# A hybrid encoder trunk in float32: seven-product pairs in one more stage, a wider attention-value product, fewer pages completed by DMA, and a new planner table

## The chip, the cores and the metric

The kernel runs on one core of a Trainium2 chip. The metric is the device time of one execution in microseconds; lower is better. Three runs of the kernel before gave 2622.74, 2623.55 and 2625.89 us, median 2623.55 us.

## The reference, cut to what matters

Two layers. In each, one input projection feeds grouped-query attention (16 query heads over 4 key/value heads) and eight bidirectional retention heads; both are gated and meet in one output projection with a residual:

```python
for l in range(DEPTH):                      # 2
    h = rmsnorm(x, norm_w[l])               # x: 256 x 4096, float32
    proj = h @ w_in[l]                      # 4096 x 11264
    aq, ak, av, ag, rq, rk, rv, rg = jnp.split(proj, SPLIT_POINTS, axis=-1)
    ...
    a_out = silu(ag) * gqa_attention(aq, ak, av)
    ...
    r_out = silu(rg) * rmsnorm(bidirectional_retention(...), ret_norm[l])
    x = x + jnp.concatenate([a_out, r_out], axis=-1) @ w_out[l]   # 4096 x 4096
return rmsnorm(x, final_norm)
```

Almost all arithmetic lies in `h @ w_in` and in the product with `w_out`; the weights, 256 rows of tokens against 4096 x 15360 numbers per layer, are read once from HBM.

## The kernel before, in words

**Stages and blocks.** Four stages follow each other: w_in of layer 0, w_out of layer 0, w_in of layer 1, w_out of layer 1 (stages 0 to 3). A w_in stage has 11 blocks, a w_out stage 4. A block makes two 512-wide column groups for all 256 tokens, so its result is a 2 x 2 arrangement of 128 x 512 tiles. The 4096 rows of the sum are taken as 16 pairs of 128-row slices.

**Products.** A pair would need eight 128 x 128 by 128 x 512 products for the 2 x 2 tiles. The pairs in `SEVEN` (0, 3, 6, 9, 12) need seven, by sums of operands and of weights (Strassen's scheme in Winograd's form, `SEVEN_PRODUCTS`); the pairs in `MORE` (before: pair 1) need seven in the w_out stages alone. All others take `EIGHT_PRODUCTS`. The partial results meet in PSUM banks M1 to M7, and `combine` (VectorE additions) puts the four tiles together at the end of a block. Blocks at the start of stage 0 counted by `PLAIN` use `PLAIN_PRODUCTS`, with an eighth bank M8; the difference operands (`third`: x3, the difference of the two token halves) are then not needed yet.

**Float32 by three products.** Every operand is split in a high part (a cast to float32r on ScalarE) and a low part (the rest, a subtraction on VectorE). A product is three matmuls: weights' high part with the operand's high and low part (line 1472), and weights' low part with the operand's high part (line 1482). `TOGETHER` products of one page run their high matmuls first, then the low ones.

**Weights.** A page is 128 x 1024 numbers of a pair. SyncE loads raw pages (`wraw`, 5 buffers); ScalarE makes `whi`, VectorE `wlo` (5 buffers each, `RING`). A seven-product pair has four pages: A, T, B, U, where T and U are sums of weights (`wsum`, one 1024-wide and two 512-wide VectorE operations per block), and B is half a page. An eight-product pair has pages A and B. For the pairs in `FAR_PAIRS` (before: 2, 5, 8, 11, 14, in every stage) page B's low part is made without VectorE: ScalarE writes `fhi` and then `flo` = -`fhi`, and GpSimd issues a DMA that adds the weights from HBM into `flo` (line 516). There is one `fhi`/`flo` buffer (`FAR = 1`), so the next far page can be begun only when the last product with the previous one is through.

**Other work.** Attention, retention, rotary embedding, the residual and the splitting of operands for the next stage are generators (`Lane`, `Turn`) whose steps are put between the products. `attention_values` (lines 1112 to 1138) is called 16 times, each for two heads.

**What sets the order.** Everything is written out at build time. After each product `tick` puts pending low parts, transfers and steps into the engines' queues if `Weights.room` says that VectorE and ScalarE will still be in time for the next pages. `room` reckons with the table at the file's head (`STEP_V`, `STEP_S`, `V_FIXED`, `PASS`, `MARGIN`, `RUSH`, `LANDING`, `ADD_AHEAD` and so on). The numbers therefore set only in which order instructions stand in each engine's queue; on the chip, semaphores alone decide when one starts.

Of the kernel before, what the change touches and what calls it, by code (L numbers as in the profile page):

```python
# [12 lines left out]
F32R = mybir.dt.float32r  # L13
# [4 lines left out]
P = 128  # L18
D_MODEL = 4096
SEQ = 256  # L20
DEPTH = 2
# [10 lines left out]
MT = SEQ // P  # L32
# [18 lines left out]
LANDING = 11.0  # L51
STORE = 7.0
FETCH = 13.0
FAR_LANDING = 11.0
MARGIN = 0.2

RUSH = 1.5

EARLY = 0.7

ADD_AHEAD = 2.5

NEED = {"ak": 4, "ag": 3, "rk": 4, "rg": 4}

PE_REST = 1.5

TIGHT_A = 4
TIGHT_B = 7

AT_ONCE = 2  # L70

WARM = 20

SPLITS = 3
# [10 lines left out]

WHOLE = 4

PLAIN = 2

DEFER = (0,)  # L90

FAR_PAIRS = (2, 5, 8, 11, 14)


AQ, AK, AV, AG, RQ, RK, RVO, RG = 0, 2048, 2560, 3072, 5120, 6144, 7168, 9216
# [95 lines left out]
    return order + rest  # L191


def is_far(group, p, k):

    return k == PAGE_B and p in FAR_PAIRS


def slots_of(group, second, first=False, plain=False):

    for _p, _k in pages_of(group, first):
        if _p in SEVENS[second] and not (first and _p in NATIVE):
# [11 lines left out]
EASY = ("M7",)  # L214


BANK_REST = 0.8
# [55 lines left out]
def hybrid_encoder(  # L273
# [136 lines left out]
    class Weights:  # L410


        def __init__(self):
            self.pages = []
            for l in range(DEPTH):
                for w, n in ((w_in, N_IN), (w_out, N_OUT2)):
                    for b in range(n):
                        second = w is w_out
                        for g in GROUPS[second]:
                            start = (l, b) == (0, 0) and w is w_in  # L420
                            for slot in slots_of(g, second, start):
# [3 lines left out]
                                one.seven = one.pair in SEVENS[second] and not one.whole  # L425
                                one.far = is_far(g, one.pair, one.kind) and not (
                                    start and (g in GROUPS[0][:2] or one.whole)
                                )
# [163 lines left out]
    def dead_room():  # L592

        if not rooms:
            e, o = len(EIGHTS), len(SEVENS[1])
# [32 lines left out]
    def split_pair(p, v, whole, stage):  # L628
# [12 lines left out]
                as_it_comes[p] = (whole, ac.until + PASS)  # L641
            yield
        x0, x1 = v[:, 0], v[:, 1]
        if p in SEVENS[stage % 2]:
# [5 lines left out]
            hi = t(ap, [P, 7, P], "x7h", len(SEVENS[1]), F32R)  # L650
            lo = t(ap, [P, 7, P], "x7l", len(SEVENS[1]), F32R)
# [16 lines left out]
        else:  # L668
            if p in EIGHTS:
                hi = t(ap, [P, 2, SEQ], "x8h", len(EIGHTS), F32R)  # L670
                lo = t(ap, [P, 2, SEQ], "x8l", len(EIGHTS), F32R)
                g = t(ap, [P, 2, 2, P], "x3", len(EIGHTS), F32R)
                g = [g[:, k] for k in range(2)]
            else:
                both = [t(ap, [P, 7, P], v, len(SEVENS[1]), F32R) for v in ("x7h", "x7l")]
# [23 lines left out]
        if p % 2:  # L699
            drop()  # L700
        version[p] += 1
        operand[p] = (hi, lo) if p in SEVENS[stage % 2] else (hi, lo, g)
        operand_at[p] = max(ve.until, ac.until) + PASS
        yield

# [264 lines left out]
        for m in range(MT):  # L970
            ve.tensor_sub(to[1][:, m], v[:, m], f32(to[0])[:, m])

    def in_both(v, i):

        return v.rearrange("p (k i t) -> p i k t", k=4 * MT, t=BLK)[:, i]

    def parts_of(name, shape):
        return page(shape, name + "h", F32R), page(shape, name + "l", F32R)

# [12 lines left out]
    def at(parts, *index):  # L992
        return [v[index] for v in parts]
# [121 lines left out]
    def attention_values(g, h, kv, sgT):  # L1115
# [17 lines left out]
        yield  # L1133
        drop(2)
        z = sgT.rearrange("p (k i t) -> p i k t", k=4 * MT, t=BLK)[:, h : h + 2]
# [225 lines left out]
    def block(after_pair, phase, then, first_order=False, order=LAST_ORDER, last=None, plain=False, hurried=False):  # L1361
# [4 lines left out]


        flat = []
        second = phase % 2 == 0
        rush[0] = RUSH if hurried else 0.0  # L1370
        for g in GROUPS[second]:
            for slot in slots_of(g, second, first_order, plain):
                flat += slot
        if plain:
            order = PLAIN_ORDER
# [22 lines left out]
        def begin_product(n, name, p, index, k, h):  # L1398
# [17 lines left out]
                acc[name] = t(pm, [P, NB], "ps" if name == "M8" else name)  # L1416
            if first_order and p in NATIVE:
                a = as_it_comes[p][0][:, index[0], index[1] * P : (index[1] + 1) * P]
            elif p in SEVENS[second]:
# [421 lines left out]
```

## Time and profile before

| what | value |
|---|---|
| median of three runs | 2623.55 us |
| span of the profiled execution, first to last instruction | 2619.4 us |
| instructions in the span | 34550 |
| TensorE matmuls | 11725 |
| HBM read, written | 637.60 MB, 44.04 MB |

The page gives the profiled execution's span alone: 4.15 us less than the median of the runs, which also hold what lies around the span. A block takes 83 to 90 us. Times in the profile are microseconds from the span's start; in the view of groups "busy" is the time covered by a group and "mean ns" the recorded length of one instruction. Recorded lengths of neighbours overlap: a 128 x 512 matmul is recorded with 389 ns, though the next one starts 227 ns after it. In the timeline a row's bracket shows the idle time before it and what ended it. In the chain of waits each row is the stretch from one piece's start to the next one's.

### The profile page before, as it was taken

How to read it: one execution, taken by the hardware profiler on the slowest of the kernel's cores; microseconds unless marked ns; L12 is line 12 of the kernel's file. 1: busy time of each engine (PE TensorE's matmuls, PEld its weight loads, DVE VectorE, ACT ScalarE, POOL GpSimd, SP SyncE). 2: the span in 40 equal slices, each digit the busy share in tenths (PEclk: the TensorE clock that was granted, in tenths of full speed). 3: DMA queues.
4: the chain of work that ended last, by engine and by line, in shares of the span. 5: the costliest groups of instructions: out<-in, count | busy, mean ns of one | idle time of the engine just before them, and what ended most of it. 6: DMA issues, size and time to landing. Idle time of an engine off the chain costs nothing.

```text
span 2619.4 us, 34550 instructions
## 1 busy us (share of the span) xinstructions
PE 2599.9 (99%) x11725; PEld 2153.7 (82%) x11725; DVE 2168.9 (83%) x2684; ACT 1805.0 (69%) x2576; POOL 373.9 (14%) x510
## 2 busy tenths in 40 slices
PE   9999999999999999999999999999999999999998
PEld 7888888888888888888878888888888888888886
DVE  8898887888778898877888878987887688987876
ACT  8766776666666788656886666776676567876555
POOL 0012221220111101111111111221110111010000
PEclk9999999999999999999999999999999999999999
DMA  8979989887878787988888888988877887788886
GB/s 306 292 257 297 284 257 287 274 270 240 247 229 258 225 252 237 283 269 269 301 251 262 271 286 268 278 270 282 280 228 218 249 259 237 224 255 270 242 261 221
DMA packets 201122, 683.95 MB, mean 261 GB/s; under 512 B 24176, under 2 KB 30832, under 8 KB 200944
## 3 DMA queue, kind: packets, MB, share of 16 engines
q1 hardware_dynamic: 147760, 521.27, 57.2%
q0 software_dynamic: 53184, 160.46, 26.3%
q8 instruction: 92, 1.51, 0.2%
q14 instruction: 86, 0.70, 0.1%
HBM read 637.60 MB, written 44.04 MB: 260 GB/s over the span
## 4 chain that ended last, share of the span: by engine, by line
PE 90%; DMA 1%; DVE 1%; issue 0%; ACT 0%; POOL 0%; POOLq 0%; DVEq 0%; ACTq 0%
PE M L1472 58%; PE M L1482 29%; PE ps L988 1%; PE ps L989 1%; PE ps L987 1%; DMA flo<-in_w_in 1%; DMA x7h<-in_w_out 0%; DVE wlo L258 0%; DVE ca L258 0%; DVE cb L258 0%; ACT flo L258 0%; ACT fhi L258 0%; ACT whi L258 0%; ACT x L258 0%; DVE xf L258 0%
## 5 line engine op out<-in xcount | busy, mean ns | idle before, releaser
L258 ACT CAST whi<-wraw 128x1024 fp32r<-128x1024 f32 (+1 forms) x808 | 768.0, 961 | 468.0 <-PE M L1472 318.7
L258 DVE TENSOR_TENSOR wlo<-wraw,whi 128x1024 fp32r<-128x1024 f32 (+1 forms) x808 | 887.6, 1110 | 234.0 <-ACT whi L258 226.2
L1472 PE MATMUL M<-whi,x8h 128*128 128x512 f32 x1340 | 521.8, 389 | 0.0
L1472 PE MATMUL M<-whi,x8l 128*128 128x512 f32 x1340 | 521.4, 389 | 0.0
L1472 PE MATMUL M<-whi,x7h 128*128 128x512 f32 x1265 | 493.2, 390 | 2.8 <-DVE ca L258 2.6
L1472 PE MATMUL M<-whi,x7l 128*128 128x512 f32 x1265 | 492.4, 389 | 0.0
L258 ACT CAST whi<-wsum 128x1024 fp32r<-128x1024 f32 x314 | 329.8, 1050 | 142.3 <-PE M L1472 109.2
L1482 PE MATMUL M<-wlo,x8h 128*128 128x512 f32 x1340 | 420.8, 389 | 0.0
L258 DVE TENSOR_TENSOR wlo<-wsum,whi 128x1024 fp32r<-128x1024 f32 x314 | 382.6, 1219 | 36.7 <-ACT whi L258 33.6
L1482 PE MATMUL M<-wlo,x7h 128*128 128x512 f32 x1265 | 408.5, 389 | 2.0 <-DVE wlo L258 2.0
L1472 PEld LDWEIGHTS M<-whi,x8l 128*128 128x128 f32 x1340 | 251.6, 188 | 52.3 <-issue 0.2
L1472 PEld LDWEIGHTS M<-whi,x8h 128*128 128x128 f32 x1340 | 251.5, 188 | 52.0 <-ACT full L258 0.2
L1482 PEld LDWEIGHTS M<-wlo,x8h 128*128 128x128 f32 x1340 | 250.5, 188 | 50.7
L1472 PEld LDWEIGHTS M<-whi,x7h 128*128 128x128 f32 x1265 | 237.5, 188 | 55.1 <-DVE ca L258 3.8
L1482 PEld LDWEIGHTS M<-wlo,x7h 128*128 128x128 f32 x1265 | 237.2, 188 | 51.6 <-DVE wlo L258 2.9
L1472 PEld LDWEIGHTS M<-whi,x7l 128*128 128x128 f32 x1265 | 237.5, 188 | 48.8
L1472 PE MATMUL M<-whi,x 128*128 128x512 f32 x840 | 258.8, 389 | 0.0
L516 POOL DMA_DIRECT2D flo<-in_w_in x108 | 96.7, 896 | 1045.3 <-ACT flo L258 965.6
L258 ACT CAST fhi<-wraw 128x1024 fp32r<-128x1024 f32 (+1 forms) x148 | 154.7, 1045 | 103.0 <-PE M L1472 97.7
L258 DVE TENSOR_TENSOR wsum<-wraw 128x1024 f32<-128x1024 f32 x157 | 191.2, 1218 | 24.2 <-DMA wraw<-in_w_out 15.6
L1472 PEld LDWEIGHTS M<-whi,x 128*128 128x128 f32 x840 | 156.9, 188 | 32.2 <-ACT whi L258 0.2
L1472 PE MATMUL M<-fhi,x8h 128*128 128x512 f32 x440 | 171.3, 389 | 0.0
(307 smaller groups left out, 3280.5 us busy)
## 6 DMA issues: line engine op xcount, KB each, us to landing
wraw<-in_w_in SPq DMA_DIRECT2D x700, 512.0 KB, 5.1
wraw<-in_w_out SPq DMA_DIRECT2D x256, 512.0 KB, 5.3
flo<-in_w_in POOLq DMA_DIRECT2D x108, 512.0 KB, 8.2
flo<-in_w_out POOLq DMA_DIRECT2D x38, 512.0 KB, 8.7
full<-next_dram POOLq DMA_DIRECT2D x18, 512.0 KB, 7.6
p_dram<-room POOLq DMA_DIRECT2D x64, 128.0 KB, 4.7
pT<-p_dram POOLq DMA_DIRECT2D x16, 512.0 KB, 5.9
next_dram<-room POOLq DMA_DIRECT2D x40, 128.0 KB, 6.8
```

Of the source, the lines that this page charges most:

```text
L258: return call(out, *args, **kwargs)
L516: nc.gpsimd.dma_start(g.lo[h], g.src[0][:, h, :], accum_op=ALU.add)
L987: nc.tensor.matmul(out, a[0], b[0], start=start, stop=False)
L988: nc.tensor.matmul(out, a[0], b[1], start=False, stop=False)
L989: nc.tensor.matmul(out, a[1], b[0], start=False, stop=stop)
L1472: nc.tensor.matmul(acc[name], a[i], g.hi[h], start=m == first[name] and not i, stop=False)
L1482: nc.tensor.matmul(acc[name], a, g.lo[h], start=False, stop=m == final[name])
```

## The change

It has four parts.

1. **Seven products.** `MORE` is pair 10 (was 1), and it takes seven products in stages 1, 2 and 3 (was: stages 1 and 3). So w_in of layer 1 now has six pairs with seven products in each of its 11 blocks; w_in of layer 0 keeps five, w_out keeps six.
2. **Attention values.** Two heads' values, before two accumulation groups of 256 columns, are one group of 512 columns: the moving operand is read as (head, 8 pieces, 32 tokens).
3. **Far pages.** `FAR_PAIRS` loses pair 5 and counts for w_in alone; w_out has far pages for pairs 5 and 14 only (`FAR_OUT`).
4. **The planner's table** is new, `PLAIN` is 1 (was 2), `TOGETHER` 3 (was 4), and `TURNS`, which deals the pages of the last group's pairs between those of pair 12, is "02".

Cut to its core (of the table some lines):

```diff
-STEP_V = 1.6
-STEP_S = 1.3
-V_FIXED = 0.15
+STEP_V = 0.8
+STEP_S = 1.5
+V_FIXED = 0.1
...
-PASS = 0.2
+PASS = 0.3
-MARGIN = 0.2
-RUSH = 1.5
+MARGIN = 0.8
+RUSH = 0.5
-ADD_AHEAD = 2.5
+ADD_AHEAD = 0.5
...
-MORE = (1,)
+MORE = (10,)
+
+MORE_IN = (1, 2, 3)
...
-PLAIN = 2
+PLAIN = 1
-FAR_PAIRS = (2, 5, 8, 11, 14)
+FAR_PAIRS = (2, 8, 11, 14)
+
+FAR_OUT = (5, 14)
...
-SEVENS = (SEVEN, tuple(sorted(SEVEN + MORE)))
-EIGHTS = [_p for _p in range(NP) if _p not in SEVENS[1]]
+SEVENS = [tuple(sorted(SEVEN + MORE)) if _s in MORE_IN else SEVEN for _s in range(2 * DEPTH)]
+EVER = sorted(SEVEN + MORE)
+EIGHTS = [_p for _p in range(NP) if _p not in EVER]
...
-def is_far(group, p, k):
-    return k == PAGE_B and p in FAR_PAIRS
+def is_far(stage, p, k):
+    return k == PAGE_B and p in (FAR_OUT if stage % 2 else FAR_PAIRS)
...
-TOGETHER = 4
+TOGETHER = 3
-TURNS = "0123"
+TURNS = "02"
...
         o = (yield from take_bank()).rearrange("p (e q) -> p e q", e=2)
-        for e in range(2):
-            for k in range(MT):
-                product(
-                    o[:, e, :].rearrange("p (k t) -> p k t", t=BLK),
-                    at(v, ALL, k),
-                    [in_both(w, 2 * e + k) for w in parts],
-                    k == 0,
-                    k == MT - 1,
-                )
+        for k in range(MT):
+            product(
+                o.rearrange("p e (k t) -> p e k t", t=BLK),
+                at(v, ALL, k),
+                [w.rearrange("p (k e j t) -> p j e k t", e=2, j=MT, t=BLK)[:, k] for w in parts],
+                k == 0,
+                k == MT - 1,
+            )
```

Two places show what moves. The first is TensorE in the fourth block, at a call of `attention_values` (`pTh` and `pTl` are the parts of the two heads' weights, `kv` the values, M the banks of the block's own products). Before, from the block's products into the call:

```order
L1472 MATMUL M_2575<-whi,x8l 128x512
L1482 MATMUL M_2548<-wlo,x_260 128x512
L987 MATMUL ps<-pTh,kv 128x256
L988 MATMUL ps<-pTl,kv 128x256
L989 MATMUL ps<-pTh,kv 128x256
```

and now:

```order
L1482 MATMUL M_2571<-wlo,x8h 128x512
L1482 MATMUL M_2554<-wlo,x_161 128x512
L988 MATMUL ps<-pTh,kv 128x512
L989 MATMUL ps<-pTl,kv 128x512
L990 MATMUL ps<-pTh,kv 128x512
```

The last three rows stand four times in a row before, and twice now: 12 matmuls of 256 columns became 6 of 512.

The second is VectorE at the end of the second block (`ca`, `cb` are the block's result tiles; M1003, M1025, M1028, M1034, M1125 and M1007 are its banks M7, M5, M4, M2, M6 and M3 in the new numbering, M993, M1030, M1015, M1018, M1094 and M997 in the old one; `ps_1009` is M8; `wlo_1708` and `wlo_1706` are the low parts of page T of pair 0 of the next block). Before:

```order
L258 TENSOR_TENSOR cb_1588<-ca_1587,M6_1094 128x512
L258 TENSOR_TENSOR ca_1587<-cb_1588,M7_993 128x512
L258 TENSOR_TENSOR cb_1588<-ca_1587,M5_1030 128x512
L258 TENSOR_TENSOR cb_1588<-cb_1588,M5_1030 128x512
L258 TENSOR_TENSOR wsum_1702<-wraw_1560,wsum_1652 128x512
L258 TENSOR_TENSOR wsum_1702<-wsum_1702,wraw_1578 128x512
L258 TENSOR_TENSOR wlo_1708<-wsum_1652,whi_1707 128x1024
L258 TENSOR_TENSOR cb_1588<-cb_1588,M3_997 128x512
L258 TENSOR_TENSOR cb_1588<-cb_1588,ps_1009 128x512
L258 TENSOR_TENSOR ca_1587<-ca_1587,M4_1015 128x512
L258 TENSOR_TENSOR wlo_1757<-wraw_1647,whi_1756 128x1024
L258 TENSOR_TENSOR ca_1587<-ca_1587,M2_1018 128x512
```

and now:

```order
L263 TENSOR_TENSOR cb_1608<-ca_1607,M6_1125 128x512
L263 TENSOR_TENSOR ca_1607<-cb_1608,M7_1003 128x512
L263 TENSOR_TENSOR wlo_1683<-wraw_1642,whi_1682 128x1024
L263 TENSOR_TENSOR wsum_1700<-wraw_1581,wsum_1668 128x512
L263 TENSOR_TENSOR wsum_1700<-wsum_1700,wraw_1599 128x512
L263 TENSOR_TENSOR wlo_1706<-wsum_1668,whi_1705 128x1024
L263 TENSOR_TENSOR akl_1717<-k_1632,akh_1716 128x4x128 x2
L263 TENSOR_TENSOR cb_1608<-cb_1608,M3_1007 128x512
L263 TENSOR_TENSOR cb_1608<-ca_1607,M5_1025 128x512
L263 TENSOR_TENSOR cb_1608<-cb_1608,M5_1025 128x512
L263 TENSOR_TENSOR ca_1607<-ca_1607,M4_1028 128x512
L263 TENSOR_TENSOR ca_1607<-ca_1607,M2_1034 128x512
```

The read of M8 is gone, the reads of M6 and M7 stand ahead of one more weight page, and between the reads of M4 and M2, where a weight page's low part stood, there is nothing now.

More of the change, by code (lines that the diff above doesn't have):

```diff
@@ L54 @@
 FAR_LANDING = 11.0
-MARGIN = 0.2
-RUSH = 1.5
+MARGIN = 0.8
+RUSH = 0.5
 EARLY = 0.7
-ADD_AHEAD = 2.5
-NEED = {"ak": 4, "ag": 3, "rk": 4, "rg": 4}
+ADD_AHEAD = 0.5
+NEED = {"ak": 4, "ag": 4, "rk": 5, "rg": 4}
 PE_REST = 1.5
-TIGHT_A = 4
-TIGHT_B = 7
+TIGHT_A = 2
+TIGHT_B = 9
 AT_ONCE = 2
 WARM = 20
-SPLITS = 3
+SPLITS = 2
 START = 1
 SEVEN = (0, 3, 6, 9, 12)
-MORE = (1,)
+MORE = (10,)
+MORE_IN = (1, 2, 3)
 DELAYED = tuple([_p for _p in range(NP) if _p not in SEVEN + MORE][-5:])
@@ L191, in pages_of, with slots_of @@
     return order + rest
-def is_far(group, p, k):
-    return k == PAGE_B and p in FAR_PAIRS
-def slots_of(group, second, first=False, plain=False):
+def is_far(stage, p, k):
+    return k == PAGE_B and p in (FAR_OUT if stage % 2 else FAR_PAIRS)
+def slots_of(group, stage, first=False, plain=False):
     for _p, _k in pages_of(group, first):
-        if _p in SEVENS[second] and not (first and _p in NATIVE):
+        if _p in SEVENS[stage] and not (first and _p in NATIVE):
             yield [(_b, _p, (ALL, _a), _k, _h) for _b, _a, _pg, _h in SEVEN_PRODUCTS if _pg == _k]
@@ L417, in __init__ @@
                     for b in range(n):
-                        second = w is w_out
-                        for g in GROUPS[second]:
+                        stage = 2 * l + (w is w_out)
+                        for g in GROUPS[stage]:
                             start = (l, b) == (0, 0) and w is w_in
-                            for slot in slots_of(g, second, start):
+                            for slot in slots_of(g, stage, start):
                                 one = Page()
@@ L424, in __init__ @@
                                 one.whole = start and one.pair in NATIVE
-                                one.seven = one.pair in SEVENS[second] and not one.whole
-                                one.far = is_far(g, one.pair, one.kind) and not (
+                                one.seven = one.pair in SEVENS[stage] and not one.whole
+                                one.far = is_far(stage, one.pair, one.kind) and not (
                                     start and (g in GROUPS[0][:2] or one.whole)
@@ L643, in split_pair @@
         x0, x1 = v[:, 0], v[:, 1]
-        if p in SEVENS[stage % 2]:
+        if p in SEVENS[stage]:
             while sums_of or held[0] + pledged() >= PAGES:
@@ L649, in split_pair @@
             sums_of.append(p)
-            hi = t(ap, [P, 7, P], "x7h", len(SEVENS[1]), F32R)
-            lo = t(ap, [P, 7, P], "x7l", len(SEVENS[1]), F32R)
+            hi = t(ap, [P, 7, P], "x7h", len(EVER), F32R)
+            lo = t(ap, [P, 7, P], "x7l", len(EVER), F32R)
             f = page([P, 5, P], "xf")
@@ L674, in split_pair @@
             else:
-                both = [t(ap, [P, 7, P], v, len(SEVENS[1]), F32R) for v in ("x7h", "x7l")]
+                both = [t(ap, [P, 7, P], v, len(EVER), F32R) for v in ("x7h", "x7l")]
                 hi, lo = (v[:, 0:4, :].rearrange("p (i m) t -> p i (m t)", m=MT) for v in both)
@@ L701, in split_pair @@
         version[p] += 1
-        operand[p] = (hi, lo) if p in SEVENS[stage % 2] else (hi, lo, g)
+        operand[p] = (hi, lo) if p in SEVENS[stage] else (hi, lo, g)
         operand_at[p] = max(ve.until, ac.until) + PASS
@@ L1368, in block @@
         flat = []
-        second = phase % 2 == 0
+        stage = phase - 1
         rush[0] = RUSH if hurried else 0.0
-        for g in GROUPS[second]:
-            for slot in slots_of(g, second, first_order, plain):
+        for g in GROUPS[stage]:
+            for slot in slots_of(g, stage, first_order, plain):
                 flat += slot
@@ L1418, in begin_product @@
                 a = as_it_comes[p][0][:, index[0], index[1] * P : (index[1] + 1) * P]
-            elif p in SEVENS[second]:
+            elif p in SEVENS[stage]:
                 a = at(operand[p], *index, ALL)
```

8 lines of the change are left out of this document (3 added, 5 removed).

## The prediction, as it was put on record

> **What bounds the kernel now.** I read the page's busy times first, then its chain of waits, then the view of waits cut to TensorE, and last the timeline of one engine at a time. The page's head and its chain:
>
> ```profile
> span 2619.4 us, 34550 instructions
> PE 2599.9 (99%) x11725; PEld 2153.7 (82%) x11725; DVE 2168.9 (83%) x2684; ACT 1805.0 (69%) x2576; POOL 373.9 (14%) x510
> PE 90%; DMA 1%; DVE 1%; issue 0%; ACT 0%; POOL 0%; POOLq 0%; DVEq 0%; ACTq 0%
> ```
>
> TensorE is busy for 99% of the span and is 90% of the chain that ended last. Busy alone proves little, since recorded matmuls overlap, so the pace has to be read from starts. Timeline of TensorE in the first block, twelve matmuls apart:
>
> ```profile
> 36.05 0.39 PE L1472 MATMUL M<-whi,x8h 128*128 128x512 f32 x1
> ...
> 38.77 0.39 PE L1472 MATMUL M<-whi,x7h 128*128 128x512 f32 x1
> ```
>
> Twelve matmuls in 2.72 us are 0.227 us each at a width of 512. The 11725 matmuls are nearly all of this kind, and 11000 times 0.227 us is 2497 us: the span is the matmuls' number times their pace, plus the start, the tail and little else. How little, the view of TensorE's waits says:
>
> ```profile
> PE M L1472 <- DVE ca L258: 2.6, 4, 1.0
> PE M L1482 <- DVE wlo L258: 2.0, 2, 1.7
> PE M L1482 <- DMA flo<-in_w_in: 0.9, 2, 0.6
> PE M L1482 <- DMA x7h<-in_w_out: 0.4, 1, 0.4
> ```
>
> Nine waits, 5.9 us between the start and the tail. Each hides another 0.16 us under the recorded end of the matmul before it (0.39 less 0.227), so about 7.4 us in all. **So a removed matmul counts in full, and everything else counts only as far as it makes or ends one of these waits.**
>
> The Trainium skill, "Trainium Kernel Development and Optimization", section "Performance Expectations", says that matmul busy time is a bad measure of the distance to the roofline and that the busy share of weight loads is a good one. By the 82% of PEld above TensorE would have room left, and taking matmuls away could gain nothing; the even spacing of starts speaks against that here.
>
> **The change part by part.**
>
> *Seven products for pair 10 in stage 2.* 11 blocks lose one product each, three matmuls of width 512: 33 x 0.227 = **-7.5 us**. The matmuls of w_out stay as many as they were, since pair 10 takes pair 1's place there. By a page of the skill ("TensorE: Matmul & The Clock Gate", section "Back-to-back issue gap") a stream with weight loads runs at about 131 ns per matmul of width 512; by that the part would be an estimated 4.3 us. The trace says 227 ns, and I keep to it.
>
> *Attention values.* A call's first matmul, its last, and the next product:
>
> ```profile
> 287.66 0.28 PE L987 MATMUL ps<-pTh,kv 128*128 128x256 f32 x1
> ...
> 288.99 0.28 PE L989 MATMUL ps<-pTh,kv 128*128 128x256 f32 x1
> 289.11 0.39 PE L1482 MATMUL M<-wlo,x8h 128*128 128x512 f32 x1
> ```
>
> Twelve narrow matmuls take 1.45 us, 0.121 each: two narrow ones cost a little more than one wide one. Six wide ones at 0.227 are 1.36, so a call saves 0.09 us and 16 calls **-1.5 us**. No row shows a wide matmul whose moving operand comes in pieces of 32 numbers; the narrow ones here read such pieces already. The nearest rows bound it: at the narrow pace it would be 6 x 0.242, a gain of nothing; at the wide pace 1.5 us. I take the wide one, as the pieces are the same. The reads of the result stay as they are.
>
> *The second block's end.* `PLAIN = 1` takes bank M8 out of the second block, and the order shows that VectorE no longer makes a weight page between the last bank reads. Today TensorE waits there twice:
>
> ```profile
> 181.72 0.50 PE L1482 MATMUL M<-wlo,x7h 128*128 128x512 f32 x1 [0.37 <-DVE wlo L258]
> 185.25 0.50 PE L1472 MATMUL M<-whi,x7h 128*128 128x512 f32 x1 [0.61 <-DVE ca L258]
> ```
>
> That is 0.98 us plus twice the hidden 0.16: **-1.3 us**, if both go. What is late next is the first block's end, since the difference operands of the second block's pairs are now made earlier: two more of them, at four short operations each, and the four reads of M6, M7 and M5 stand ahead of the boundary instead of behind it. It may lose what the other gains (bounds 0 and 2.6 us, twice today's); I take nothing.
>
> *Far pages.* In w_out three of five far pages become near ones. The one wait of the last block for such a transfer goes with them:
>
> ```profile
> 2583.33 0.50 PE L1482 MATMUL M<-x7h,x8h 128*128 128x512 f32 x1 [0.40 <-DMA x7h<-in_w_out]
> ```
>
> 0.40 plus 0.16: **-0.6 us**. In w_in of layer 1 the seven products of pair 10 put the far pages of pairs 8 and 11 nearer together. Counted in the order, 52 matmuls lie between the last use of the one and the first of the other at six places (at the others tasks' matmuls stand between); before, the least in w_in was 66. In that time the single buffer must be filled anew, and the chain of waits shows what this takes:
>
> ```profile
> flo<-in_w_in POOLq DMA_DIRECT2D x108, 512.0 KB, 8.2
> 940.32 9.58 DMA flo<-in_w_in
> ...
> 1364.71 1.06 ACT fhi L258
> 1365.77 0.02 issue
> 1365.80 1.07 ACT flo L258
> 1366.86 0.29 issue
> 1367.15 7.42 DMA flo<-in_w_in
> ```
>
> Two casts and the issue are 2.44 us, the landing 8.2 in the median: 10.6 against 52 x 0.227 = 11.8 us. With a landing of 9.58 it is 12.0, and 0.2 us late; behind another cast on ScalarE, 1 us more. Behind TensorE's waiting matmul stands everything, so a late landing counts whole. Between nothing and 2 us at each of six places, I take 0.3: **+1.8 us**. Today's two waits for `flo`, 0.9 us and twice 0.16, have 66 matmuls; they shift with the order and I let them fall: **-1.2 us**.
>
> *More work on VectorE.* Starts of neighbours give its prices:
>
> ```profile
> 84.71 1.22 DVE L258 TENSOR_TENSOR wsum<-wraw 128x1024 f32<-128x1024 f32 x1
> 85.85 1.22 DVE L258 TENSOR_TENSOR wlo<-wraw,whi 128x1024 fp32r<-128x1024 f32 x1
> 86.99 0.42 DVE L258 TENSOR_TENSOR x<-x3f,x 128x256 fp32r<-128x256 f32 x1
> ...
> 91.22 0.69 DVE L258 TENSOR_TENSOR cb<-ca,M 128x512 f32<-128x512 f32 x1
> 91.82 0.68 DVE L258 TENSOR_TENSOR cb<-cb,M 128x512 f32<-128x512 f32 x1
> ```
>
> 1.14 us for 1024 numbers, 0.60 for 512. A near page instead of a far one adds 1.14. A pair with seven products has low parts of 3.5 pages instead of 2 (4.0 us instead of 2.3) and weight sums of 1.14 + 0.60 + 0.60: 4.1 more. Per block that is +1.1 us in stage 0, +5.2 in stage 2, +3.4 in w_out. The cover is VectorE's idle time; view of windows, a block to a row (DVE is the third pair of numbers), and one heavy stretch:
>
> ```profile
> 27.20:95.20 68.00, 68.00 (x301) 56.31 (x300) 61.77 (x88) 56.93 (x94) 3.62 (x4) 1.00 0.90 300
> 95.20:180.10 84.90, 84.30 (x371) 69.14 (x370) 78.48 (x132) 58.04 (x91) 12.85 (x16) 1.00 0.87 264
> 884.90:973.60 88.70, 88.38 (x407) 73.50 (x406) 81.27 (x126) 72.59 (x120) 12.38 (x12) 1.00 0.79 247
> 973.60:1059.40 85.80, 85.80 (x391) 71.53 (x390) 77.14 (x103) 69.72 (x112) 7.52 (x8) 1.00 0.75 235
> 1225.40:1308.30 82.90, 82.90 (x367) 68.66 (x366) 74.66 (x108) 69.42 (x116) 14.13 (x21) 1.00 0.89 292
> 1567.00:1656.50 89.50, 89.50 (x419) 75.03 (x417) 74.72 (x88) 63.51 (x99) 18.16 (x28) 1.00 0.86 269
> 2183.30:2271.30 88.00, 88.00 (x406) 73.46 (x405) 80.16 (x124) 72.41 (x120) 12.43 (x12) 1.00 0.78 249
> 2271.30:2357.90 86.60, 86.17 (x391) 71.50 (x390) 78.21 (x105) 69.92 (x112) 7.54 (x8) 1.00 0.74 232
> 960.00:980.00 20.00, 20.00 (x93) 16.66 (x92) 19.86 (x30) 12.13 (x15) 0.86 (x1) 1.00 0.74 218
> ```
>
> An ordinary block of stage 2 (1567) has 14.8 us idle and takes 5.2. The two blocks around the end of stage 2 (2183 and 2271) have 7.8 + 8.4 = 16.2 idle and take 8.6, so VectorE would stand at 96% there for 174 us. The last row shows that it can be 99% busy for 20 us while TensorE loses nothing. The price lies between nothing and what the rival below pays; near the row at 99% I take **+2 us**. ScalarE loses a cast of 1.07 us with each far page and is the less full one in every block above. The transfers become fewer.
>
> *The table.* It moves instructions within the queues and adds none. The worst place today is the seam of stages 1 and 2, where both waits for `wlo` and `ca` of over 1 us lie; the bank reads stand there in the same sequence, so I leave those waits in.
>
> **Sum.** -7.5 - 1.5 - 1.3 - 0.6 + 1.8 - 1.2 + 2 = -8.3 us. Against the span: 2619.4 - 8.3 = 2611.1. The runs' median stands 4.15 us above that span; with it **2615.3 us**.
>
> **The rivals.**
> 1. *VectorE becomes the bound (slower).* Its idle time in the heavy blocks is not slack but waiting for ScalarE's casts in a strict order, and cannot be given up. Then each added microsecond lands on TensorE wherever VectorE is at 90% or more: the blocks above at 884, 973, 1225, 2183 and 2271 add 1.1 + 3.4 + 3.4 + 5.2 + 3.4 = 16.5, and the first two blocks (27 and 95) 2.3, 18.8 in all. 2623.55 - 9.0 + 18.8 = 2633.4. It decides from the point where VectorE needs more than the 4% that are left around 2271. For it: the added work sits just there. Against: the stretch at 99%. Chance 0.10.
> 2. *New waits eat the gain (no change).* The six `flo` places cost up to 2 us each and the seams of the stages one or two more: 8 more than I take, 2623. Chance 0.22. That the removed matmuls were hidden anyway, as the share of weight loads would have it, gives the same 2623.5 and is in this chance.
> 3. *The new order also ends the waits that I left in.* The larger `MARGIN` puts low parts earlier; then hardly a wait is left: 2623.55 - 9.0 - 7 = 2607.5. Chance 0.18.
>
> **How the numbers follow.** My forecast, 2611 to 2618, has 0.50. 0.2% (5.2 us) is about what a measurement of this kernel can tell from no change: faster means under 2618.3, slower over 2628.8. Forecast and third rival make faster 0.68, the second rival same 0.22, the first slower 0.10. The range goes from the third rival's time to a little beyond the second's, 2607.5 to 2626: it leaves out most of the slower case and the best few runs of the third.
>
> **What would show it.** The count of matmuls must fall by 129, to 11596, and the starts stay 0.227 us apart; the timeline at a call of `attention_values` must show six rows in 1.36 us. The wait at the second block's end is gone. New rows "PE M <- DMA flo<-in_w_in" between 1350 and 2270 us would show the far pages' price, rows "PE M <- DVE wlo" or "<- DVE ca" near 2250 VectorE's. The prediction is wrong if the waits of TensorE outside start and tail sum to more than 12 us, or if the wide product runs at another pace.

## The result, and the profile after

The changed kernel takes **2619.56 us** in the median of 21 runs (2616.31 to 2621.03); the kernel before, run beside it, 2622.92 us (21 runs, 2620.67 to 2625.89). The ratio is 0.9984 with a 95% interval of 0.9978 to 0.9990. That is 3.4 us less: clear of the noise, but within the 0.2% that the prediction called no change, and 4.3 us more than the 2615.3 it gave.

The head of the page of the kernel after:

```profile
span 2618.4 us, 34300 instructions
PE 2595.2 (99%) x11596; PEld 2142.3 (82%) x11596; DVE 2257.9 (86%) x2786; ACT 1774.0 (68%) x2552; POOL 325.7 (12%) x464
PE 92%; DMA 3%; DVE 2%; ACT 2%; issue 1%; SPq 0%; DVEq 0%; POOLq 0%; POOL 0%; ACTq 0%
```

The 129 matmuls are gone, VectorE has 89 us more work, and the shares of DMA, VectorE and ScalarE in the chain have grown from 2% together to 7%. What TensorE waits for after (total us, times, longest; `junk` belongs to the warm-up ahead of the first product, `pTl` is the low part of two heads' attention weights, `D` a step of the retention; two rows of 0.6 us are left out):

```profile
PE M L1472 <- ACT whi L263: 2.1, 2, 1.1
PE ps L988 <- DVE D L263: 1.8, 1, 1.8
PE M L1482 <- DMA flo<-in_w_in: 1.3, 1, 1.3
PE M L1472 <- DVE cb L263: 1.3, 1, 1.3
PE ps L1705 <- DVE junk L263: 1.1, 1, 1.1
PE ps L989 <- DVE pTl L263: 0.9, 1, 0.9
PE M L1472 <- DVE ca L263: 0.8, 3, 0.3
```

None of the old long rows (`wlo`, `ca`, `x7h`) is left at its length; others stand in their place, and more of them.

To make a full account I took the distance between starts of neighbouring matmuls from the first product on, and subtracted the pace: 0.2268 us for a wide one, 0.120 for a narrow one, 0.238 for a wide one of the attention values. What is left is waiting, the hidden 0.16 us and any stretch at a lower clock included.

| | before | after |
|---|---|---|
| start, to the first product | 21.4 us | 19.6 us |
| matmuls at their pace | 2575.4 us | 2567.8 us |
| waits | 10.5 us | 18.5 us |
| tail, from the last matmul | 12.1 us | 12.6 us |
| span | 2619.4 us | 2618.4 us |
| waits in 0 to 200 us | 3.5 us | 8.0 us |
| waits in 900 to 1400 us | 5.3 us | 3.6 us |
| waits in 1700 to 1900 us | 0 us | 2.1 us |
| waits in 2200 to 2300 us | 0.7 us | 4.7 us |

**In these two executions the matmuls gave 7.6 us of the 9.0 forecast, and 8.0 us more of waits took them back.** More than half of these, 4.5 us, lie before 200 us. The start is a matter of the execution, not of the change: in two of the 14 profiles here the full clock is granted at 9.8 and 9.9 us and the start takes 21.4 us, in the others at 4.0 to 7.0 us, and it takes 19.2 to 19.9.

The account is of one execution each, and these two lie on opposite sides of their medians. A run's time stands 2.1 us above its span before and 1.8 us after, so only 2.1 of the 4.15 us named ahead of the prediction lie around the span; the other 2 are a profiled execution that was faster than the median run. Median spans are 2620.8 us before (15 runs beside experiment 1) and 2617.8 after: 3.0 us less, where the two profiled spans differ by 1.0. With the matmuls' 7.6 us and 0.5 us more of tail, the waits of a median run grew by some 4 us rather than 8, if its start is the same in both kernels (an estimate from these numbers).

The heaviest place is at 2257 us. Timeline of TensorE (start, length, instruction, in brackets the idle time before it and what ended it):

```profile
2257.20 0.39 PE L988 MATMUL ps<-rkqh 128*128 128x256 f32 x1 [1.75 <-DVE D L263]
2258.24 0.96 PE L1472 MATMUL M<-whi,x 128*128 128x512 f32 x2
2259.00 0.63 PE L1472 MATMUL M<-whi,x8h 128*128 128x512 f32 x1
2259.43 0.63 PE L1472 MATMUL M<-whi,x8l 128*128 128x512 f32 x1
```

and of VectorE ahead of it:

```profile
2245.07 1.22 DVE L263 TENSOR_TENSOR wlo<-wraw,whi 128x1024 fp32r<-128x1024 f32 x1 [1.21 <-ACT whi L263]
...
2254.66 0.41 DVE L263 TENSOR_TENSOR x7l<-full,x7h 128x256 fp32r<-128x256 f32 x1
2254.99 1.22 DVE L263 TENSOR_TENSOR wlo<-wraw,whi 128x1024 fp32r<-128x1024 f32 x1
2256.13 0.42 DVE L263 TENSOR_TENSOR x<-full,x 128x256 fp32r<-128x256 f32 x1
2256.46 0.68 DVE L263 SCALAR_TENSOR_TENSOR D<-ps,D 128x512 f32<-128x512 f32 x1
```

`D` stands behind a packed queue that lost 1.21 us at 2245.07 to a cast. TensorE waits 1.9 us for it in all, and then the wide matmuls start 0.43 us apart instead of 0.23, for 3.41 us: the granted clock was 0.5 there. The wait cost 1.9 us and the clock another 1.7.

The cast was late because its raw page was. ScalarE:

```profile
2243.98 1.06 ACT L263 CAST whi<-wraw 128x1024 fp32r<-128x1024 f32 x1 [4.51 <-DMA wraw<-in_w_in]
```

SyncE asked for this page at 2236.07 us, when VectorE had finished the last low part from its buffer (2236.05), and it landed 7.80 us later. ScalarE's waits for raw pages of w_in, and the median landing of such a page, before:

```profile
ACT whi L258 <- DMA wraw<-in_w_in: 37.4, 22, 4.5
...
wraw<-in_w_in SPq DMA_DIRECT2D x700, 512.0 KB, 5.1
```

and after:

```profile
ACT whi L263 <- DMA wraw<-in_w_in: 105.9, 50, 7.3
...
wraw<-in_w_in SPq DMA_DIRECT2D x700, 512.0 KB, 5.0
```

The waits have nearly trebled while the landing is the same, not only in the median: 127 of the 700 pages took over 7 us before, 129 after. A raw buffer is free when VectorE has made its last low part or sum from it, so a fuller VectorE lets pages be asked for later, and then the slower landings come too late: 41 of the 50 waits after are for pages that took over 5.1 us, as the one above. Had no page taken more than 5.0 us, 43 of the 105.9 us would be left, and 9 of the 37.4 before (an estimate from the issues and landings of these pages).

### The profile page after: what moved, and what is told of

Read it like the earlier page. It is cut to its first block, busy times and chain, and to the rows that moved or that the text cites. A ratio compares the mean times of both kernels' runs of the same rounds, so it can differ in the third digit from the quotient of the medians.

```text
span 2618.4 us, 34300 instructions
## 1 busy us (share of the span) xinstructions
PE 2595.2 (99%) x11596; PEld 2142.3 (82%) x11596; DVE 2257.9 (86%) x2786; ACT 1774.0 (68%) x2552; POOL 325.7 (12%) x464
## 4 chain that ended last, share of the span: by engine, by line
PE 92%; DMA 3%; DVE 2%; ACT 2%; issue 1%; SPq 0%; DVEq 0%; POOLq 0%; POOL 0%; ACTq 0%
PE M L1472 59%; PE M L1482 29%; DMA wraw<-in_w_in 2%; DVE wlo L263 1%; PE ps L989 1%; PE ps L988 1%; PE ps L990 1%; ACT whi L263 1%; DMA flo<-in_w_in 0%; PE M L1466 0%; DMA ca<-in_x 0%; DVE wsum L263 0%; ACT to L263 0%; PE ps L1472 0%; DMA fhi<-in_w_in 0%
## 5 line engine op out<-in xcount | busy, mean ns | idle before, releaser
L263 ACT CAST whi<-wraw 128x1024 fp32r<-128x1024 f32 (+1 forms) x853 | 808.8, 960 | 476.3 <-PE M L1472 284.1
L263 DVE TENSOR_TENSOR wlo<-wraw,whi 128x1024 fp32r<-128x1024 f32 (+1 forms) x853 | 929.5, 1107 | 155.5 <-ACT whi L263 146.6
L1472 PE MATMUL M<-whi,x8h 128*128 128x512 f32 x1467 | 572.6, 390 | 0.8 <-DVE ca L263 0.8
L1472 PE MATMUL M<-whi,x8l 128*128 128x512 f32 x1467 | 571.5, 390 | 0.0
L1482 PE MATMUL M<-wlo,x8h 128*128 128x512 f32 x1467 | 505.0, 389 | 0.0
L263 DVE TENSOR_TENSOR wlo<-wsum,whi 128x1024 fp32r<-128x1024 f32 x336 | 409.5, 1219 | 70.6 <-ACT whi L263 63.0
L1482 PEld LDWEIGHTS M<-wlo,x8h 128*128 128x128 f32 x1467 | 275.7, 188 | 57.1
L1472 PE MATMUL M<-whi,x 128*128 128x512 f32 x960 | 296.2, 390 | 1.1 <-ACT whi L263 1.1
L1482 PE MATMUL M<-wlo,x 128*128 128x512 f32 x480 | 187.2, 390 | 0.4 <-DVE wlo L263 0.4
L263 ACT CAST fhi<-wraw 128x1024 fp32r<-128x1024 f32 (+1 forms) x103 | 107.9, 1048 | 88.8 <-PE M L1472 88.6
```

The source lines that it names most:

```text
L263: return call(out, *args, **kwargs)
L1472: nc.tensor.matmul(acc[name], a[i], g.hi[h], start=m == first[name] and not i, stop=False)
L1482: nc.tensor.matmul(acc[name], a, g.lo[h], start=False, stop=m == final[name])
```

## The experiments

Each is compared with the kernel before, run beside it (its median lay between 2622.2 and 2624.3 us). "Waits" are those of the account above, again of one execution each. A seam is the place where one stage ends and the next begins.

**1. Two plain blocks again.** The changed kernel with

```diff
-PLAIN = 1
+PLAIN = 2
```

> The changed kernel with two plain blocks again instead of one; all else as changed. Theory A: the waits of TensorE in the first 200 us, 8.0 us in the changed kernel's profile against 3.5 before, come with the single plain block (difference operands and bank reads come earlier, and transfers of the start fall together). Then they fall to about 3.5 and the time to 2615. Theory B: they come with the new table and from late raw pages whatever the number of plain blocks. Then the time stays within 1 us of 2619.6.

Measured: 2622.24 us, ratio 0.9995 (0.9986 to 1.0004); waits 21.9 us, of which 11.2 lie before 200 us. The early waits did not go, so the single plain block is not their cause. As Theory B said, they stay; the time is 2.7 us above the changed kernel's, more than it allowed, though the two intervals overlap.

**2. The old table on the new structure.**

```diff
-STEP_V = 0.8
+STEP_V = 1.6
...
-MARGIN = 0.8
+MARGIN = 0.2
-RUSH = 0.5
+RUSH = 1.5
...
-TOGETHER = 3
+TOGETHER = 4
-TURNS = "02"
+TURNS = "0123"
```

(and all other numbers of the table but `PLAIN`).

> The changed kernel's products, far pages and one plain block with the old planner table. Theory A: the added VectorE work makes the new waits near 2250 us (4.7 us there after, 0.7 before), so they stay with the old table: 2619 to 2622. Theory B: the new table makes them: the removed matmuls then come through nearly whole, about 2615.

Measured: 2671.25 us, ratio 1.0185 (1.0171 to 1.0199), waits 67.6 us. The same work and the same 11596 matmuls take 52 us longer; neither theory came near. TensorE's waits:

```profile
PE M L1472 <- ACT x L263: 20.5, 3, 8.9
PE M L1472 <- DVE x7l L263: 10.6, 3, 5.6
PE M L1472 <- DVE x L263: 4.7, 4, 4.0
```

These are not weights but operands of the next stage, late at the seams. The clock is at a half for 41 us in all around these waits. In 14 of them TensorE is idle anyway; the other 27 cost some 14 us of the loss.

**3. Seven products alone.** The kernel before with

```diff
-MORE = (1,)
+MORE = (10,)
+MORE_IN = (1, 2, 3)
```

and the rest as it was.

> The kernel before with one part alone: pair 10 instead of pair 1, with seven products in stages 1, 2 and 3; old table, old far pages, two plain blocks, narrow attention values. Additive theory: 33 matmuls at 0.227 us, 7.5 us less than before, 2615.4. Rival: 4 us more VectorE work per block of stage 2 turn into waits at that stage's end, which take back half or more: 2618.5 or later.

Measured: 2642.21 us, ratio 1.0081 (1.0067 to 1.0095), waits 39.6 us: the part that forecast and account put at -7.5 us makes the kernel 19 us slower by itself.

```profile
PE M L1473 <- DVE x L263: 8.8, 3, 4.4
PE M L1473 <- ACT x L263: 6.1, 3, 3.8
```

The direction is the rival's, the size is not. The waits are at the seams: 5.5 us between 1000 and 1100 us, 9.6 between 1300 and 1400, 11.3 between 2300 and 2400.

**4. Wide values from a contiguous operand.** The changed kernel with

```diff
-[w.rearrange("p (k e j t) -> p j e k t", e=2, j=MT, t=BLK)[:, k] for w in parts]
+[w.rearrange("p (j e k t) -> p j e k t", e=2, j=MT, t=BLK)[:, k] for w in parts]
```

It leaves out the regrouping of the weights' columns; each matmul reads 512 numbers in one piece.

> The changed kernel, but the wide product of the attention values reads its moving operand as 512 numbers in a row instead of 16 pieces of 32, so it multiplies other columns: the regrouping of the heads' weights is left out. The wide matmuls start 0.237 to 0.240 us apart in the changed kernel, the other wide ones 0.227. Theory A: the pieces make the difference, and the pace becomes 0.227. Theory B: it is the bank or the stationary operand; the pace stays 0.238.

Measured, one run: 2621.41 us. What it decides is the pace. Timeline of TensorE in the changed kernel:

```profile
278.79 0.40 PE L988 MATMUL ps<-pTh,kv 128*128 128x512 f32 x1
...
280.21 0.39 PE L1472 MATMUL M<-whi,x8h 128*128 128x512 f32 x1
```

and with the contiguous operand:

```profile
278.66 0.39 PE L988 MATMUL ps<-pTh,kv 128*128 128x512 f32 x1
...
280.02 0.39 PE L1472 MATMUL M<-whi,x8h 128*128 128x512 f32 x1
```

Six take 1.42 us in pieces of 32 numbers and 1.36 contiguous: 0.237 against 0.227 each. As its order is otherwise the changed kernel's, it is also a second look at the waits: 20.5 us (with 0.227 us for its attention values), among them again those before 200 and near 2258 us.

**5. The table alone.** The kernel before with the new table, but two plain blocks, the old far pages, pair 1 in `MORE` and narrow values.

> The kernel before with the new table alone: old pairs, old far pages, two plain blocks, narrow attention values. The old table on the changed structure gave 2671, 52 us more than the new one there. Theory A: the new table is needed only where VectorE has more to do; on the old structure at most today's 7 us of waits can go, and it comes to 2618 to 2624. Theory B: the table itself is the gain and the structure adds nothing: 2619.6 or less.

Measured: 2641.31 us, ratio 1.0059 (1.0046 to 1.0071), waits 32.5 us. Neither theory holds: the very numbers that are worth 52 us on the new structure cost 17 on the old one. The waits are of another kind:

```profile
PE M L1483 <- DMA flo<-in_w_in: 8.0, 6, 3.3
PE M L1483 <- DVE wlo L263: 5.9, 5, 1.9
...
PE M L1483 <- DMA flo<-in_w_out: 3.2, 3, 1.6
```

At the longest of these waits, at 146 us, the far buffer was free at 128.5, but ScalarE began the far page's cast at 134.3, behind other steps that the new order had put there, and the transfer was issued at 137.2.

**6. Pair 10 with eight products in stage 2.** The changed kernel with

```diff
-MORE_IN = (1, 2, 3)
+MORE_IN = (1, 3)
```

> The changed kernel without the seventh product pair in stage 2 (w_in of layer 1 has five such pairs again); all else as changed. Additive theory: 33 matmuls at 0.227 us come back, 2619.6 + 7.5 = 2627. Theory A: the 4 us of VectorE work per block that go too take the waits near 2250 us and some at the seams with them, so it comes to 2622 to 2624.

Measured: 2619.68 us, ratio 0.9987 (0.9979 to 0.9996), so the same as the whole change, though 33 matmuls (7.5 us) come back: Theory A's way, and further than it said. Its waits are 12.3 us instead of 18.5; after 1200 us, 1.9 instead of 9.7. In stage 2, this is all that TensorE waits for (1309 to 2270 us):

```profile
PE M L1472 <- DVE ca L263: 0.3, 1, 0.3
```

In the changed kernel four waits stand there, 3.4 us in sum, those for `D` and `pTl` among them. ScalarE's waits for raw pages go the same way, 63.7 us in place of 105.9, in part because fewer pages landed late (92 of 700 took over 7 us, 129 in the changed kernel):

```profile
ACT whi L263 <- DMA wraw<-in_w_in: 63.7, 29, 9.5
```

This is the run that shows where the forecast gain went: what pair 10 saves in stage 2 on TensorE, it gives back in the same stage, up to its end. The medians say so without any profile: 7.5 us of matmuls more, and the time is 0.1 us longer.

**7. The old far pages.** The changed kernel with

```diff
-FAR_PAIRS = (2, 8, 11, 14)
+FAR_PAIRS = (2, 5, 8, 11, 14)
-FAR_OUT = (5, 14)
+FAR_OUT = (2, 5, 8, 11, 14)
```

> The changed kernel with the far pages of before (2, 5, 8, 11, 14 in every stage): 3 low parts fewer for VectorE in each w_out block, 1 fewer in each w_in block, and as many more transfers into the one buffer. Theory A: VectorE's load makes the waits; they fall by 3 us or more, 2616 or less. Theory B: late raw pages and late additions by DMA make them; more transfers make it 2620 to 2625.

Measured: 2644.99 us, ratio 1.0083 (1.0069 to 1.0096), waits 42.2 us, 19.4 of them between 1700 and 1800 and between 1900 and 2000 us. Neither theory's time came; with this table and these pairs, fewer far pages are a condition of the gain.

**8. Six numbers of the table.** The changed kernel with `STEP_V`, `STEP_S`, `V_FIXED`, `PASS`, `MARGIN` and `RUSH` as before.

> The changed kernel with six numbers of the old table: STEP_V, STEP_S, V_FIXED, PASS, MARGIN, RUSH, those by which the planner decides whether a step may go into the queues. With the whole old table the operands of the next stage came late at every seam (waits for x, x3 and x7, 60 us with the clock's halving). Theory A: these six do it, and the time is 2650 to 2670. Theory B: the rest does it (three splittings at a time instead of two, the pages that tasks ask for, the tight ends), and the time stays within 5 us of 2619.6.

Measured: 2660.16 us, ratio 1.0138 (1.0122 to 1.0153), waits 57.0 us. This is Theory A: these six alone lose 41 us of the table's 52. They decide when `room` lets a step in. The waits are again for operands:

```profile
PE M L1472 <- ACT x L263: 17.3, 3, 9.3
PE M L1472 <- DVE x L263: 6.1, 5, 3.6
```

**9. Fewer far pages in w_out alone.** The kernel before with `FAR_OUT = (5, 14)`.

> The kernel before with one part alone: two far pages instead of five in the w_out stages; all else old. Theory A (each part alone upsets an order that its own table had been fitted to): slower than before, 2630 or more, with waits for operands at the seams, as the seven products alone (2642) and the table alone (2641) had. Theory B (fewer far pages help by fewer transfers: 683.95 MB before, 660.34 after): 2623 or less.

Measured: 2647.58 us, ratio 1.0101 (1.0086 to 1.0117), waits 36.9 us: Theory A. The first of its two longest waits shows what happens at a seam. TensorE:

```profile
1055.44 0.80 PE L1473 MATMUL M<-whi,x 128*128 128x512 f32 x1 [6.96 <-ACT x L263]
```

ScalarE:

```profile
1047.92 2.94 ACT L263 CAST whi<-wraw 128x1024 fp32r<-128x1024 f32 x3
1050.76 1.71 ACT L263 ACTIVATE ca<-ca,nw 128x256 f32<-128x256 f32 x4
1052.37 1.31 ACT L263 CAST x8h<-ca 128x256 fp32r<-128x256 f32 x4
1054.98 0.41 ACT L263 CAST x<-ca 128x256 fp32r<-128x256 f32 x1 [1.30 <-DVE ca L263]
```

and VectorE:

```profile
1045.30 1.23 DVE L263 TENSOR_TENSOR wlo<-wraw,whi 128x1024 fp32r<-128x1024 f32 x1 [2.67 <-ACT whi L263]
1048.06 1.23 DVE L263 TENSOR_TENSOR wlo<-wsum,whi 128x1024 fp32r<-128x1024 f32 x1 [1.53 <-ACT whi L263]
...
1051.47 2.35 DVE L263 TENSOR_TENSOR wlo<-wraw,whi 128x1024 fp32r<-128x1024 f32 x2
...
1054.53 0.42 DVE L263 TENSOR_TENSOR ca<-ca 128x256 f32<-128x256 f32 x1
```

The operand `x` that TensorE stands for is made from a short operation on VectorE (1054.53), which is queued behind weight pages, and these behind casts on ScalarE. VectorE was idle for 4.2 us just before. So nothing here is short of throughput; the order is. That the old numbers, told of more work on VectorE, let the operands' steps in too late is my reading, which experiment 8 supports.

**10. Longer rests for steps.** An attempt at something better than both: the changed kernel with

```diff
-PE_REST = 1.5
+PE_REST = 3.0
...
-BANK_REST = 1.0
+BANK_REST = 2.5
```

so that TensorE comes later to a step that waits for VectorE, as `D` and `pTl` do.

> The changed kernel with PE_REST 3.0 instead of 1.5 and BANK_REST 2.5 instead of 1.0: the tasks' own products are put later into TensorE's queue behind the VectorE work that they wait for. In the profile TensorE stands 1.75 us at 2255 for a bank that VectorE reads late (1.7 us more by the halved clock) and 1.2 us at 1777 for a low part of the heads' weights. Theory A: these two waits are the planner's, and go: 5 us less, 2615. Theory B: any change of a number reshuffles the queues, and other waits come: 2619 or more.

Measured: 2624.14 us, ratio 1.0006 (0.9998 to 1.0015), waits 23.2 us: Theory B. The waits for `D` and `pTl` went, and others of the same size came (2.2 us for a `flo` at 2246 us, again with 3.41 us at the half clock). The waits moved with the order; giving these steps more time did not make them fewer.

**11. Narrow values.** The changed kernel with the two accumulation groups of 256 columns as before.

> The changed kernel with the two narrow products per call as before. Six wide matmuls 0.238 us apart are 1.43 us, twelve narrow ones 1.45: by the pace the time moves by 0.3 us. Additive theory: 2619 to 2620.5. Rival: the planner reckons the narrow ones a little longer, the order changes, and the time with it by 2 us or more either way.

Measured: 2619.62 us, ratio 0.9992 (0.9983 to 1.0001): the wide product is worth nothing that can be measured.

**12. Pair 5 a far page in w_in.** The changed kernel with

```diff
-FAR_PAIRS = (2, 8, 11, 14)
+FAR_PAIRS = (2, 5, 8, 11, 14)
```

> The changed kernel with pair 5 a far page again in w_in alone (both layers); w_out keeps far pages for pairs 5 and 14 only. It takes 1.14 us of work from VectorE in each of 22 blocks and gives ScalarE one cast of 1.07 us more. Theory C, the added waits after 1200 us come from VectorE being too full in stage 2: VectorE has 12.5 us less work there, so the waits after 1200 us fall from 9.7 to 5 us or less, and the time is 2615 to 2617 us if nothing else moves. Theory D, the single flo buffer has no room for a fifth far page beside six pairs with seven products: rows of TensorE waiting for a flo transfer appear in stage 2, 5 us or more in sum, and the time is over 2625. With pair 5 far in w_in and w_out the time was 2645, so the run also says which of the two stages' far pages made that: near 2645 it is w_in's, near 2620 w_out's.

Measured: 2639.42 us, ratio 1.0061 (1.0047 to 1.0075), waits 39.8 us. Theory D's time and rows (5.0 us in stage 2), not C's: relief for VectorE by this way makes it worse, and most of experiment 7's loss is w_in's. The largest `flo` wait, on TensorE:

```profile
1724.83 1.22 PE L1482 MATMUL M<-flo,x8h 128*128 128x512 f32 x2 [4.32 <-DMA flo<-in_w_in]
```

and its transfer, on GpSimd:

```profile
1709.22 0.55 POOL L1181 DMA_DIRECT2D next_dram<-sgT  x1 [18.03 <-DVE sgT L263]
1709.76 0.56 POOL L1161 DMA_DIRECT2D kv<-kv_dram  x1
1710.29 0.56 POOL L955 DMA_DIRECT2D q<-q_dram  x1
1710.82 0.95 POOL L521 DMA_DIRECT2D flo<-in_w_in  x1
```

Three other transfers were issued in the 1.6 us ahead of it, each 512 KB, and it landed 13.96 us after its issue where the median is 7.9. Even so issued, a median landing would have come at 1718.7 us, before TensorE needed it (1720.3, behind its last matmul with `fhi`). So D's reason, too many far pages for one buffer, is not that of this wait; a far page also shares its queue with attention's transfers. The longest wait of the run is of yet another kind, for a bank at a block's end:

```profile
1938.80 0.80 PE L1472 MATMUL M<-whi,x7h 128*128 128x512 f32 x1 [6.20 <-DVE ca L263]
```

From 1928.1 to 1937.4 us VectorE's queue held steps of the rotary embedding, and the two bank reads that TensorE needed stood behind them. This again is order and not throughput. The run says nothing on whether VectorE's fullness as such makes the waits of stage 2, since it put other waits in their place.

## Why the prediction was right or wrong, point by point

The time lies in the stated range (2607.5 to 2626 us), but above the forecast of 2611 to 2618; the range holds it because it reached over the second rival, to which the prediction gave 0.22. In its own terms the matmuls were to give 9.0 us and gave 7.6; all the other terms together were to cost 0.7 us and cost some 4 in a median run, and 8.0 by the two profiled executions. So the direction came out right by the matmuls; that the time lies in the range is owed to the range's width and not to the sum.

- *Seven products, -7.5 us.* Right on TensorE: the pace stayed at 0.227 us, and the matmuls' part of the account fell by 7.6 us. The Trainium skill's 131 ns ("TensorE: Matmul & The Clock Gate", "Back-to-back issue gap") shows nowhere here.
- *Attention values, -1.5 us.* Mis-sized: a wide matmul with pieces of 32 numbers runs at 0.237 us, nearly the narrow bound of 0.242. A call takes 1.42 us, not 1.36; 16 calls save at most 0.5. "The pieces are the same" was the failed reason; the prediction had named the narrow pace as its other bound.
- *The second block's end, -1.3 us.* Wrong: before, 0.53, 0.37 and 0.77 us were lost there; after, 0.31 and 1.58 (the row `PE M <- DVE cb`). Experiment 1 shows that two plain blocks do not do better now. Before 200 us the waits grew by 4.5 us, for which the sum had no term beside this one.
- *Far pages.* The wait for `x7h` went as forecast (-0.6). The price of the six places, +1.8, did not come: no row for `flo` stands in stage 2. The two old waits for `flo`, 1.2 us, went, but one of 1.5 us came in the first block, where a landing took 11.16 us.
- *More work on VectorE, +2 us.* **This is the step that failed most**: "near the row at 99% I take +2 us". The amount of work was right. Stage 2, 1309 to 2270 us, before:

```profile
1309.00:2270.00 961.00, 957.65 (x4364) 797.11 (x4364) 796.50 (x972) 664.87 (x943) 151.14 (x207) 1.00 0.84 260
```

  after:

```profile
1309.00:2270.00 961.00, 957.41 (x4300) 792.17 (x4299) 851.56 (x1045) 669.03 (x965) 139.56 (x198) 1.00 0.80 255
```

  and without the seven products there (experiment 6):

```profile
1309.00:2270.00 961.00, 960.69 (x4334) 798.06 (x4333) 810.89 (x992) 661.40 (x954) 139.16 (x198) 1.00 0.80 254
```

  55 us more (third pair of numbers), 5.0 a block against the 5.2 forecast. The price was not 2: from 1200 us on, the waits are 9.7 us with pair 10's seven products in stage 2 and 1.9 without, 7.8 us for 41 us of VectorE's work (7.4 by the medians). Against the kernel before they grew by 3.5 us only, from 6.2, since the waits at the seam of stages 1 and 2 had shrunk (the next item). The forecast leaned on a single stretch of 20 us at 99% and took a price near nothing. The stretch shows that VectorE can be full while every page is early; it does not show what happens when raw pages are asked for later and an operation like `D` must be made between the pages. That the late raw pages are the way from the fuller VectorE to the waits is read from the rows at 2245 to 2257 us and from ScalarE's waits, not isolated by a run of its own: a run with one more raw buffer would do that, and it was not tried. Nor does experiment 6 part the amount of VectorE's work from the order that the planner gives it, which changed with it.
- *The table, 0.* Also failed: that the table "moves instructions within the queues and adds none" was taken to mean that it is worth nothing. It is worth 52 us on the new structure (experiment 2), and -17 on the old one (5). The waits at the seam of stages 1 and 2, "left in" by the forecast, shrank from 3.4 us at 1311 to 1316 us to 0.5.
- *The rivals.* The second, new waits that eat the gain, is what happened in kind, but not at its place (not the six `flo` places), and the time lies midway between the forecast and this rival's 2623. Its other reading, that the removed matmuls were hidden anyway, is refuted by the 7.6 us that they gave. The first (VectorE's work lands whole on TensorE, 18.8 us) did not happen; VectorE was given 89 us more, and all of TensorE's waits together grew by 8. The third, no waits left, is refuted by the 18.5 us.
- *What was named as refuting it.* Another pace of the wide product came true. Waits over 12 us between start and tail did by the account, 18.5 us. By the rows of the view and 0.16 us for each, from which the prediction had its 7.4 us, they are 8.8 + 11 x 0.16 = 10.6 us, and 12.3 with the 1.7 us of the half clock, which such rows do not show.

Put alone into the kernel before, the seven products cost 19 us, fewer far pages in w_out 25, the table 17; the wide values, taken out of the whole, make no difference. Together they give -3.4. Their effects don't add, since each one's price lies in waits that the others make or remove.

Open: what makes the waits before 200 us (3.5 us before, 8.0 after). Not `PLAIN` (experiment 1) and not stage 2 (9.2 us in experiment 6); the table alone has 9.7 there and the old table on the new structure 11.3, so neither the new table nor the new structure is needed for them. What TensorE waits for there is one far page (1.5 us, behind the landing of 11.16 us), two casts on ScalarE (1.3 and 1.2 us) and the bank read at the second block's end (1.6 us).

## What to carry to other kernels

When a change adds work to the second fullest engine, price it by the waits that the fuller queue makes (which input is asked for later, which short operation now stands behind long ones), and not by one stretch in which that engine was full and nothing waited. A planner's table is tuned to one structure: judge the structure and the table together, since each alone can lose several times what both gain. Take out each part again once the whole is measured; here the part that carried the forecast turned out to be worth nothing inside the whole. And give a landing its spread, not its median: the pages that came too late were mostly the slower ones.

## What the runs showed of the hardware

**A wait of 2 us can cost nearly 4.** Behind some waits of TensorE the granted clock is 0.5 for 3.41, 6.83 or 10.24 us, with wide matmuls starting 0.43 us apart. The window of the changed kernel around such a wait (the number after the engines' busy times is the granted clock):

```profile
2255.00:2264.00 9.00, 7.25 (x28) 5.61 (x28) 8.70 (x13) 8.10 (x15) 0.00 (x0) 0.81 0.92 311
```

Waits of 4 to 9 us went with 6.83 or 10.24 us at the half clock, which could begin within the wait; one of 4.79 us (experiment 2, at 2359 us) went with 3.41. Below 3 us it went both ways: waits of 1.92, 2.03 and 2.18 us (changed kernel, experiments 4 and 10) were followed by it; 1.93 us in experiment 1, 1.84 us in the kernel before and even 2.96 us in experiment 6 (at 131 us) were not. The shortest single one that was followed by it took 1.58 us (experiment 11, at 185 us), and the same wait in the changed kernel was not; two of 1.3 and 1.5 us within 2 us were (experiment 3, at 96 us). The Trainium skill ("TensorE: Matmul & The Clock Gate", "What's actually happening") gives a free-running window of 3413 ns, and the lengths here are its multiples. Its advice to avoid idle gaps over about 3 us ("Why this matters for your kernels") is too mild by these runs: it would let the waits of 1.58 to 2.18 us pass.

**Pieces cost.** A 512-wide matmul whose moving operand comes in 16 pieces of 32 numbers takes 0.237 us, contiguous 0.227 (experiment 4).

**An accumulating transfer lands late behind others of its queue:** 13.96 us after three of 512 KB, where the median is 7.9 (experiment 12), and 13.39 us behind the same three a second time in that run, at 1822 us. In all 14 profiles, no far page of w_in that was issued with no other 512 KB transfer of its queue on the way took over 11.5 us.
